# The level decays of a chunked recurrence: products of block decays in place of exponentials of differences of a running sum

## The chip, the cores and the metric

One core of one Trainium2 chip runs the whole program. The metric is the device time of one execution in microseconds, the median of several runs; before the change it is 2116.34 us, the median of 3 runs (2110.68 to 2116.36).

## The reference

Two transformer blocks run on 512 tokens of width 1024: a first block with sparse attention, latent attention and a gated feed-forward, and a second block of two layers. The change touches the first layer of the second block, an HGRN2 mixer with 8 heads of 128 key and 128 value dimensions. Cut to what matters:

```
log_f = log_sigmoid(f) ;  k = sigmoid(-f) ;  q = silu(q)          # lb is zero for this layer
per chunk of 128 frames, per head:
    b = cumsum(log_f)                                              # running sum of log decays
    scores[t, s] = sum_d q[t, d] * exp(b[t, d] - b[s, d]) * k[s, d]    for s <= t, else 0
    o = (q * exp(b)) @ state + scores @ v
    state = exp(b_last) * state + (k * exp(b_last - b))^T @ v
o = rms_norm(o) * silu(g), then @ w_out
```

The decay depends on the dimension d as well as on t and s, so the scores are no plain product of two matrices.

## The kernel before, in words

Every tile has features or dimensions on the 128 partitions and the 512 tokens on the free axis. Weights are float32 and are split into a high part on ACT (`whi`, line 431) and a rest on DVE (`wlo`, line 435); every dense product is three matmuls (`mm3`, line 481). `take` (line 443) issues the split of a block of weights three blocks ahead (`LOOK_SPLIT`) and its DMA five ahead.

The scores of a chunk are built by levels h = 64, 32, 16, 8, 4, 2, 1. At level h the tokens form pairs of blocks of length h, and the level covers the queries of a pair's second block against the keys of its first. There the decay is a product of two factors that meet at the middle of the pair, exp(b[t] - b[mid]) on the query and exp(b[mid] - b[s]) on the key, so that a matmul over d gives the scores. The diagonal needs no decay.

`hz` (line 1941) takes the projections of a head: for `f` it makes `zf` (the key), and a scan on DVE (line 1950, with the mask `scan` that is loaded at line 1926) makes the running sum `b`. `hrec` (line 1975) then does a head. It makes `kd` = k exp(b_last - b) (POOL line 1982, ACT 1984, DVE 1985), `eb` = exp(b) (ACT 1987) and `qe` = q exp(b) (DVE 1989); four matmuls `ps<-zq,zf` for the diagonal go through a predicated copy into the score tile `sc` (line 1994). `kd` is transposed on PE (line 2000) and copied back by ACT (2001). Then come the seven levels, the largest first, all from `b`, `k` and `q`. `level` (line 2005) has two subtractions on POOL (2027, 2028; one for h = 1, 2012), one exponential on ACT (2029; 2013) and two multiplications on DVE (2030, 2031; 2014, 2015) into a tile `lx`. `levmm` (line 2034) has four matmuls `ps<-lx` (one against a tile of ones for h = 1) and puts the result into `sc`, with ACT copies for h = 64 and 32 (2049, 2054) and predicated copies on DVE otherwise (2056). `vi,kd` makes the states (`st`, line 2077, scaled by a column of `eb`), `vi,sc` and `st,qe` the output of the head, and `qe` is used once more for the normalised output.

The order of the work: `hrec` is a generator that yields after each level; two of them (even and odd heads) are woven with the generator `hgrn_dense` of projections by the rates of `RATE_H` (`weave_g`, line 261). A scheduler of the framework then orders each engine's queue. Tiles of 128x512 come from a list of free slots, first in first out (`get`, `put`, lines 302 and 316).

Of the kernel before, what the change touches and what calls it, by code (L numbers as in the profile page):

```python
# [19 lines left out]
P = 128  # L20
T = 512
# [54 lines left out]
def _constants():  # L76
# [30 lines left out]
    sm = np.ones((P, T), np.float32)  # L107
    sm[:, ::P] = 0.0
    c["c_scan"] = sm
# [834 lines left out]
def _emit(s):  # L944
# [980 lines left out]
    scanm = s.get("scan")  # L1925
    nc.sync.dma_start(scanm, A["c_scan"])
# [48 lines left out]
    def hrec(hd):  # L1975
        q, k, b, g = (qfg.pop((hd, n)) for n in "qkbg")
# [12 lines left out]
        V.tensor_tensor(qe, eb, q, op=ALU.mult)  # L1989
# [15 lines left out]
        def level(i, h):  # L2005
            nb = T // (2 * h)
            x = s.get("lx")
            b4, k4, q4 = (y.rearrange("p (n e t) -> p n e t", e=2, t=h) for y in (b, k, q))
            if h == 1:
                x0 = x[:, 0:256]  # L2010
                x3 = x0.rearrange("p (n t) -> p n t", t=1)
                G.tensor_tensor(x3, b4[:, :, 1, :], b4[:, :, 0, :], op=ALU.subtract)
                S.activation(x0, x0, AF.Exp)
                V.tensor_tensor(x3, x3, k4[:, :, 0, :], op=ALU.mult)
                V.tensor_tensor(x3, x3, q4[:, :, 1, :], op=ALU.mult)
                lev[i] = x
                return
            mid = b4[:, :, 0, h - 1:h].to_broadcast([P, nb, h])
            if h == 32:
                x5 = x.rearrange("p (b e n t) -> p e b n t", b=NT, e=2, n=2)  # L2020
                x4 = [x5[:, e] for e in range(2)]
                v5 = lambda y: y.rearrange("p (b n) t -> p b n t", b=NT)
            else:
                x5 = x.rearrange("p (n e t) -> p e n t", e=2, t=h)
                x4 = [x5[:, e] for e in range(2)]
                v5 = lambda y: y
# [5 lines left out]
            lev[i] = x  # L2032

        def levmm(i, h):
            x = lev.pop(i)
            ps = s.ps()
            if h == 1:
                s.mm(ps[:, 0:256], s.ones, x[:, 0:256], True, True)
            for tb in range(NT if h > 1 else 0):
                xb = x[:, tb * P:(tb + 1) * P]  # L2040
                if h >= 32:
                    s.mm(ps[0:64, 64 * tb:64 * tb + 64], xb[:, 0:64], xb[:, 64:128], True, True)
                else:
                    r = xb.rearrange("p (n e t) -> p n e t", e=2, t=h)[:, :, 1, :]
                    s.mm(ps[:, 64 * tb:64 * tb + 64].rearrange("p (n t) -> p n t", t=h), xb, r, True, True)
# [41 lines left out]
        s.put(kd, eb, st, q, k, b)  # L2087
# [55 lines left out]
    s.put(rbc, scanm, *SC, *VI[0], *VI[1], *masks)  # L2143
# [286 lines left out]
```

## Time and profile before

| | before |
|---|---|
| median of 3 runs | 2116.34 us |
| the profiled execution's own time | 2109.22 us |
| its span | 2107.4 us |
| mean granted clock of TensorE, of full speed | 0.989 |
| PE busy | 2064.9 us (98%) |
| DVE busy | 1641.5 us (78%) |
| ACT busy | 1170.4 us (56%) |
| POOL busy | 138.5 us (7%) |

The span is the time from the first to the last instruction that the profiler saw; the own time has what lies around it. PE are matmuls, PEld their weight loads, DVE VectorE, ACT ScalarE, POOL GpSimd, SP the engine that issues most DMAs. A busy share is one of the whole span and hides stages with other limits. The HGRN stage's recurrence lies between 865 and 1140 us.

### The profile page before, as it was taken

To read this page: it belongs to the slowest core of one execution; us is meant where nothing else is said; L and a number is where in the kernel's file an instruction comes from. 1 tells how busy PE (TensorE), PEld (TensorE's weight loads), DVE (VectorE), ACT (ScalarE), POOL (GpSimd) and SP (SyncE) were. 2 spreads that over 40 slices of the span, in tenths; PEclk is the share of its full clock that TensorE was granted. 3 is DMA by queue.
4 is the path that set the end of the run, shared out by engine and by line. 5 is a ranking of instruction groups with operands and counts; after the bars stand their busy time and mean duration, and the time that the engine had idled before them with its cause. 6 is when DMAs were issued, how large, how long until landed. Compare 5 with 4: busy or idle time off the path is not lost.

```text
span 2107.4 us, 30853 instructions
## 1 busy us (share of the span) xinstructions
PE 2064.9 (98%) x11194; PEld 1748.6 (83%) x11194; DVE 1641.5 (78%) x3285; ACT 1170.4 (56%) x2174; POOL 138.5 (7%) x256
## 2 busy tenths in 40 slices
PE   9999999999999999899989999999999999999998
PEld 8788877988888889798878988888888879888886
DVE  7786698799687897977996967667887677666768
ACT  5565676465444474645664645445656565554453
POOL 0000001100000000422440000000000000000000
PEclk9999999999999999999999999999999999999999
DMA  7123166433424252222122442343563433434342
GB/s 229 41 61 100 58 176 222 155 122 106 142 91 139 101 170 91 86 70 71 61 91 90 150 159 101 131 140 112 193 201 112 141 124 114 148 109 153 108 139 92
DMA packets 106359, 258.22 MB, mean 123 GB/s; under 512 B 10944, under 2 KB 31280, under 8 KB 106208
## 3 DMA queue, kind: packets, MB, share of 16 engines
q1 hardware_dynamic: 106208, 256.27, 36.8%
q8 instruction: 88, 1.44, 0.3%
q14 instruction: 63, 0.52, 0.1%
HBM read 227.61 MB, written 24.16 MB: 119 GB/s over the span
## 4 chain that ended last, share of the span: by engine, by line
PE 47%; DVE 5%; POOL 2%; issue 1%; ACT 1%; DMA 1%; SPq 0%; DVEq 0%; POOLq 0%; ACTq 0%
PE ps L479 45%; POOL lx L2028 1%; POOL lx L2027 1%; DVE wlo L435 1%; PE s L479 1%; PE o L479 1%; DMA dtab<-rexp 1%; PE rms L479 0%; DVE lx L2030 0%; DVE lx L2031 0%; DMA raw<-in_mup 0%; ACT whi L431 0%; DVE p L2313 0%; DVE rt L684 0%; DVE xr L1758 0%
## 5 line engine op out<-in xcount | busy, mean ns | idle before, releaser
L479 PE MATMUL ps<-ah,whi 128*128 128x512 f32 (+1 forms) x1812 | 677.3, 375 | 1.8 <-ACT whi L431 1.2
L479 PE MATMUL ps<-al,whi 128*128 128x512 f32 (+1 forms) x1812 | 670.5, 370 | 1.9 <-DVE al L641 1.4
L479 PE MATMUL ps<-ah,wlo 128*128 128x512 f32 (+1 forms) x1812 | 668.1, 369 | 0.0
L431 ACT CAST whi<-raw 128x1024 fp32r<-128x1024 f32 (+3 forms) x283 | 280.4, 995 | 302.2 <-PE ps L479 286.6
L435 DVE TENSOR_TENSOR wlo<-raw,whi 128x1024 fp32r<-128x1024 f32 (+3 forms) x283 | 332.7, 1178 | 137.9 <-ACT whi L431 137.2
L479 PEld LDWEIGHTS ps<-ah,whi 128*128 128x128 f32 x1812 | 341.0, 189 | 59.8 <-ACT whi L431 1.8
L479 PEld LDWEIGHTS ps<-ah,wlo 128*128 128x128 f32 x1812 | 341.1, 188 | 59.3 <-DVE wlo L435 0.2
L479 PEld LDWEIGHTS ps<-al,whi 128*128 128x128 f32 x1812 | 341.8, 189 | 57.3 <-DVE al L641 2.3
L479 PE MATMUL ps<-whi,ah 128*128 128x512 f32 (+2 forms) x816 | 291.7, 358 | 2.1 <-DVE am L871 1.5
L479 PE MATMUL ps<-wlo,ah 128*128 128x512 f32 (+2 forms) x816 | 290.6, 356 | 1.4 <-DVE wlo L435 1.4
L479 PE MATMUL ps<-whi,al 128*128 128x512 f32 (+2 forms) x816 | 290.2, 356 | 0.0
L479 PEld LDWEIGHTS ps<-whi,ah 128*128 128x128 f32 x816 | 154.5, 189 | 27.2 <-DVE am L871 1.7
L479 PEld LDWEIGHTS ps<-wlo,ah 128*128 128x128 f32 x816 | 154.8, 190 | 26.0 <-DVE wlo L435 2.2
L479 PEld LDWEIGHTS ps<-whi,al 128*128 128x128 f32 x816 | 154.5, 190 | 23.9
L431 ACT CAST whi<-t 128x1024 fp32r<-128x1024 f32 x66 | 67.9, 1029 | 95.6 <-DVE t L394 56.0
L873 ACT ACTIVATE p<-p,am 128x128 f32<-128x128 f32 (+3 forms) x160 | 88.5, 554 | 37.1 <-DVE am L871 36.1
L435 DVE TENSOR_TENSOR wlo<-t,whi 128x1024 fp32r<-128x1024 f32 x66 | 79.0, 1198 | 38.4 <-ACT whi L431 34.7
L637 ACT CAST ah<-u 128x512 fp32r<-128x512 f32 x97 | 59.6, 619 | 46.3 <-DVE u L1720 30.1
L435 DVE TENSOR_TENSOR wlo<-b,whi 128x1024 fp32r<-128x1024 f32 (+1 forms) x44 | 52.5, 1197 | 35.4 <-ACT whi L431 35.4
L479 PE MATMUL ps<-ah,wh 128*128 128x256 f32 x256 | 73.1, 285 | 0.0
L1667 DVE TENSOR_TENSOR C<-C,ps 128x512 f32<-128x512 f32 x112 | 72.5, 681 | 0.7 <-PE ps L479 0.7
L696 DVE TENSOR_TENSOR ss<-ss,sq 128x512 f32<-128x512 f32 (+1 forms) x90 | 51.8, 575 | 27.0 <-ACT sq L695 25.7
(359 smaller groups left out, 3322.1 us busy)
## 6 DMA issues: line engine op xcount, KB each, us to landing
raw<-in_mup SPq DMA_DIRECT2D x64, 512.0 KB, 3.3
raw<-in_mdn SPq DMA_DIRECT2D x64, 512.0 KB, 3.2
raw<-in_up SPq DMA_DIRECT2D x44, 512.0 KB, 4.2
b<-in_mdn SPq DMA_DIRECT2D x32, 512.0 KB, 3.3
raw<-in_win SPq DMA_DIRECT2D x26, 512.0 KB, 3.8
raw<-in_awin SPq DMA_DIRECT2D x24, 512.0 KB, 3.2
raw<-in_down SPq DMA_DIRECT2D x20, 512.0 KB, 3.3
xsp<-x SPq DMA_DIRECT2D x32, 256.0 KB, 2.3
```

The lines of the kernel that those rows point to most:

```text
L431: self.whi_ins = self.nc.scalar.copy(hi[:, :e], raw[:, :e])
L435: eng.tensor_tensor(lo[:, d], raw[:, d], hi[:, d], op=ALU.subtract)
L479: self.nc.tensor.matmul(ps, l, r, start=first, stop=last, skip_group_check=skip)
L637: nc.scalar.copy(hi, src)
L696: nc.vector.tensor_tensor(ss[:, c], ss[:, c], t[:, c], op=ALU.add)
L873: nc.scalar.activation(d, d, AF.Exp, scale=-1.0, bias=m[:, qb:qb + 1], accum_out=sm[:, qb:qb + 1])
L1667: V.tensor_tensor(C[i, j, tb], C[i, j, tb], pss[tb], op=ALU.add)
L2027: G.tensor_tensor(x4[1], v5(b4[:, :, 1, :]), v5(mid), op=ALU.subtract)
L2028: G.tensor_tensor(x4[0], v5(mid), v5(b4[:, :, 0, :]), op=ALU.subtract)
```

## The change

The running sum `b` is gone, with its scan, its mask (a constant, a load and a tile), and every exponential of a difference. `hz` keeps `f` itself, exp(log_f), in the tile `ls`. `hrec` builds up from the smallest level. The decays of blocks come from DVE: `dec[2h]` is the product of neighbouring pairs of `dec[h]`, seven products of 256, 128, ..., 4 elements into a tile `dt` (line 1990 of the changed kernel). Two running operands start as K = k and Q = f q. At each level h, K's first block of a pair is multiplied by the decay of the second block and Q's second block by the decay of the first (DVE, lines 2004 and 2005, into new tiles `Kd` and `Qd`), and the other halves are copied by ACT (lines 2006, 2007). The matmuls of a level (`ps<-Qd,Kd`) use K and Q as they were ahead of its step; at h = 32 the weights are 96 columns (before: 64). After the level 64 K is k exp(b_last - b) and Q is q exp(b), so that the separate `kd`, `eb` and `qe` go; the transposes of K (line 2051) and their copy (2053) now stand behind the last level. The level h = 1 has a product `x1` of its own (line 1993). POOL has no work left in the recurrence.

```
@@ _constants, loads
-    sm = np.ones((P, T), np.float32)
-    sm[:, ::P] = 0.0
-    c["c_scan"] = sm
...
-    scanm = s.get("scan")
-    nc.sync.dma_start(scanm, A["c_scan"])
@@ hz
             S.activation(z, z, AF.Exp)
-            b = s.get("b")
-            V.tensor_tensor_scan(b, scanm, e, 0.0, ALU.mult, ALU.add)
-            qfg[hd, "k"], qfg[hd, "b"] = z, b
+            S.activation(e, e, AF.Exp)
+            qfg[hd, "k"], qfg[hd, "f"] = z, e
@@ hrec
-        kd = s.get("kd")
-        b3 = b.rearrange("p (a t) -> p a t", a=NT)
-        G.tensor_tensor(kd.rearrange("p (a t) -> p a t", a=NT), b3[:, :, P - 1:P].to_broadcast([P, NT, P]), b3,
-                        op=ALU.subtract)
-        S.activation(kd, kd, AF.Exp)
-        V.tensor_tensor(kd, kd, k, op=ALU.mult)
-        eb = s.get("eb")
-        S.activation(eb, b, AF.Exp)
-        qe = s.get("qe")
-        V.tensor_tensor(qe, eb, q, op=ALU.mult)
...
-        kps = s.ps()
-        for tb in range(3):
-            c = slice(tb * P, (tb + 1) * P)
-            nc.tensor.transpose(kps[:, c], kd[:, c], s.ident)
-        S.copy(kd[:, 0:384], kps[:, 0:384])
-        s.pput(kps)
-        lev = {}
+        K, Q = k, s.get("Qd")
+        V.tensor_tensor(Q, f, q, op=ALU.mult)
+        s.put(q)
+        dt = s.get("dt")
+        dec, o = {1: f}, 0
+        for h in (1, 2, 4, 8, 16, 32, 64):
+            n = T // (2 * h)
+            dec[2 * h] = dt[:, o:o + n]
+            d3 = dec[h].rearrange("p (n e) -> p n e", e=2)
+            V.tensor_tensor(dec[2 * h], d3[:, :, 0], d3[:, :, 1], op=ALU.mult)
+            o += n
+        x1 = s.get("x1")
+        V.tensor_tensor(x1[:, 0:256], k[:, 0::2], Q[:, 1::2], op=ALU.mult)
+        yield
+        lev = deque()
...
-            G.tensor_tensor(x4[1], v5(b4[:, :, 1, :]), v5(mid), op=ALU.subtract)
-            G.tensor_tensor(x4[0], v5(mid), v5(b4[:, :, 0, :]), op=ALU.subtract)
-            S.activation(x, x, AF.Exp)
-            V.tensor_tensor(x4[0], x4[0], v5(k4[:, :, 0, :]), op=ALU.mult)
-            V.tensor_tensor(x4[1], x4[1], v5(q4[:, :, 1, :]), op=ALU.mult)
-            lev[i] = x
+            V.tensor_tensor(k2[:, :, 0, :], kb[:, :, 0, :], d3[:, :, 1:2].to_broadcast([P, nb, h]), op=ALU.mult)
+            V.tensor_tensor(q2[:, :, 1, :], qb[:, :, 1, :], d3[:, :, 0:1].to_broadcast([P, nb, h]), op=ALU.mult)
+            S.copy(k2[:, :, 1, :], kb[:, :, 1, :])
+            S.copy(q2[:, :, 0, :], qb[:, :, 0, :])
+            lev.append((h, K, Q))
+            K, Q = K2, Q2
...
-                    s.mm(ps[0:64, 64 * tb:64 * tb + 64], xb[:, 0:64], xb[:, 64:128], True, True)
+                    e = P - h
+                    s.mm(ps[0:e, 64 * tb:64 * tb + 64].rearrange("p (n t) -> p n t", t=h), kb[:, c][:, 0:e],
+                         q4[:, :, 1, :], True, True)
...
-        hs = (64, 32, 16, 8, 4, 2, 1)
-        for i, h in enumerate(hs):
-            level(i, h)
+        for i, h in enumerate((1, 2, 4, 8, 16, 32, 64)):
+            level(h)
             if i:
-                levmm(i - 1, hs[i - 1])
+                levmm()
             yield
+        s.put(f)
+        kps = s.ps()
+        for tb in range(3):
+            c = slice(tb * P, (tb + 1) * P)
+            nc.tensor.transpose(kps[:, c], K[:, c], s.ident)
+        kd, qe = K, Q
+        S.copy(kd[:, 0:384], kps[:, 0:384])
+        s.pput(kps)
...
-        levmm(6, 1)
+        levmm()
...
-            V.scalar_tensor_tensor(st[:, tb * P:(tb + 1) * P], st[:, (tb - 1) * P:tb * P], eb[:, tb * P + P - 1:tb * P + P],
+            V.scalar_tensor_tensor(st[:, tb * P:(tb + 1) * P], st[:, (tb - 1) * P:tb * P], dec[128][:, tb:tb + 1],
```

How the queues stand. First DVE in the opening, where the first head's levels begin; before, the level multiplications of head 0 in their order (`zf` is the key, `zq` the query):

```order
L1985 TENSOR_TENSOR kd<-kd,zf 128x512
L1938 SCALAR_TENSOR_TENSOR ls<-zf,ls 128x512
L1989 TENSOR_TENSOR qe<-eb,zq 128x512
L1947 TENSOR_TENSOR zf<-ls,zf 128x512
L1950 SCALAR_TENSOR_TENSOR b<-scan,ls 128x512
L2030 TENSOR_TENSOR lx<-lx,zf 128x4x64
L2031 TENSOR_TENSOR lx<-lx,zq 128x4x64
L2030 TENSOR_TENSOR lx<-lx,zf 128x4x64
L2031 TENSOR_TENSOR lx<-lx,zq 128x4x64
L435 TENSOR_TENSOR wlo<-raw,whi 128x1024
```

and after the change, the same place:

```order
L1990 TENSOR_TENSOR dt<-dt 128x64
L2004 TENSOR_TENSOR Kd<-zf,ls 128x256
L1990 TENSOR_TENSOR dt<-dt 128x32
L2005 TENSOR_TENSOR Qd<-Qd,ls 128x256
L1990 TENSOR_TENSOR dt<-dt 128x16
L2004 TENSOR_TENSOR Kd<-Kd,dt 128x128x2
L1990 TENSOR_TENSOR dt<-dt 128x8
L2005 TENSOR_TENSOR Qd<-Qd,dt 128x128x2
L1990 TENSOR_TENSOR dt<-dt 128x4
L2038 COPY_PREDICATED sc<-mask,ps 128x256
L432 TENSOR_TENSOR wlo<-raw,whi 128x1024
```

The small products `dt` stand between the multiplications of the first two levels, and each level's multiplication now reads the tile that the level ahead of it wrote.

Second ACT, somewhat later, where both heads' levels run; before:

```order
L1984 ACTIVATE kd<-kd 128x512
L1987 ACTIVATE eb<-b 128x512
L2029 ACTIVATE lx<-lx 128x512 x2
L431 CAST whi<-raw 128x1024
L2001 COPY kd<-ps 128x384
L2029 ACTIVATE lx<-lx 128x512 x2
```

and after:

```order
L2053 COPY Kd<-ps 128x384
L2006 COPY Kd<-Kd 128x32x8
L2007 COPY Qd<-Qd 128x32x8
L2006 COPY Kd<-Kd 128x16x16
L2007 COPY Qd<-Qd 128x16x16
L428 CAST whi<-raw 128x1024
L2006 COPY Kd<-Kd 128x8x32
L2007 COPY Qd<-Qd 128x8x32
```

Two copies of half the size stand where one exponential stood, and a weight cast can stand between the copies of one level and the next.

Third PE at head 6, near the end of the stage; before, where the levels 16 to 2 of that head follow each other without dense matmuls (`ident,qe` are transposes of another head's output, `vi,sc` its score product):

```order
L479 MATMUL ps<-lx 128x64 x16
L479 MATMUL ps<-vi,kd 128x128 x3
L479 MATMUL ps<-lx,ones 128x256
L2106 MATMUL ps<-ident,qe 128x128 x2
L479 MATMUL ps<-zq,zf 128x128 x2
```

and after:

```order
L476 MATMUL ps<-Qd,Kd 128x64 x12
L476 MATMUL ps<-Qd,Kd 96x64 x4
L2051 MATMUL ps<-ident,Kd 128x128 x3
L476 MATMUL ps<-Qd,Kd 64x64 x4
L476 MATMUL ps<-zq,zf 128x128
L476 MATMUL ps<-vi,Kd 128x128 x3
L2095 MATMUL ps<-ident,Qd 128x128 x4
```

The transposes of `Kd` moved behind the last level, and five matmuls stand between them and `vi,Kd`, which reads their copy.

## Rows read from the trace of the kernel before

**Rows 1.** The page's busy times: engine, us, share of the span, instructions.
```profile
PE 2064.9 (98%) x11194; PEld 1748.6 (83%) x11194; DVE 1641.5 (78%) x3285; ACT 1170.4 (56%) x2174; POOL 138.5 (7%) x256
```
**Rows 2.** Busy time by stretch: length, PE, PEld, DVE, ACT, POOL, granted clock, DMA share, GB/s.
```profile
865.00:1140.00 275.00, 259.48 (x1609) 226.74 (x1609) 231.54 (x451) 158.70 (x335) 102.40 (x112) 0.95 0.21 70
870.00:900.00 30.00, 22.69 (x149) 20.53 (x148) 29.97 (x38) 18.75 (x37) 26.69 (x28) 0.80 0.07 24
1050.00:1080.00 30.00, 27.07 (x135) 22.89 (x134) 27.96 (x59) 20.82 (x41) 6.82 (x8) 0.89 0.20 71
1080.00:1110.00 30.00, 26.09 (x156) 21.44 (x155) 29.31 (x58) 19.62 (x43) 15.47 (x17) 0.95 0.35 115
1110.00:1125.00 15.00, 15.00 (x102) 13.49 (x102) 12.36 (x40) 4.95 (x17) 3.38 (x4) 0.88 0.30 88
```
**Rows 3.** PE timeline: start, us, line, operation, [idle before and what ended it].
```profile
876.24 0.52 PE L2000 MATMUL ps<-ident,kd 128*128 128x128 f32 x3 [1.62 <-DVE kd L1985]
882.41 1.11 PE L479 MATMUL ps<-lx 128*64 128x64 f32 x8 [1.96 <-DVE lx L2031]
...
1056.39 1.22 PE L479 MATMUL ps<-vi,sc 128*128 128x128 f32 x4 [2.93 <-DVE sc L2056]
...
1106.79 1.22 PE L479 MATMUL ps<-lx,ones 128*128 128x256 f32 x2 [3.69 <-DVE sc L2056]
```
**Rows 4.** DVE and POOL timelines around 896 us, POOL's last subtraction of heads 0 and 1.
```profile
894.42 0.83 DVE L2031 TENSOR_TENSOR lx<-lx,zq 128x256 f32<-128x256 f32 x1
895.18 0.42 DVE L2056 COPY_PREDICATED sc<-mask,ps 128x256 f32<-128x256 uint32 x1
...
898.24 0.41 DVE L2030 TENSOR_TENSOR lx<-lx,zf 128x256 f32<-128x256 f32 x1
898.57 0.41 DVE L2031 TENSOR_TENSOR lx<-lx,zq 128x256 f32<-128x256 f32 x1
...
896.44 0.79 POOL L2012 TENSOR_TENSOR lx<-b 128x256 f32<-128x256 f32 x1
```
**Rows 5.** Groups of DVE instructions, 865 to 1140 us: count | busy us, mean ns | idle before.
```profile
L435 DVE TENSOR_TENSOR wlo<-raw,whi 128x1024 fp32r<-128x1024 f32 x28 | 38.0, 1357 | 4.8 <-ACT whi L431 4.6
L2030 DVE TENSOR_TENSOR lx<-lx,zf 128x256 f32<-128x256 f32 x48 | 28.1, 586 | 0.6 <-ACT lx L2029 0.6
L2031 DVE TENSOR_TENSOR lx<-lx,zq 128x256 f32<-128x256 f32 x48 | 26.3, 548 | 0.0
L1950 DVE TENSOR_TENSOR_SCAN b<-scan,ls 128x512 f32<-128x512 f32 x8 | 10.1, 1267 | 0.0
L1985 DVE TENSOR_TENSOR kd<-kd,zf 128x512 f32<-128x512 f32 x8 | 7.3, 916 | 0.1
```
**Rows 6.** Groups of DVE instructions, 600 to 868 us, where POOL does no subtraction.
```profile
L435 DVE TENSOR_TENSOR wlo<-raw,whi 128x1024 fp32r<-128x1024 f32 x36 | 44.0, 1222 | 14.8 <-ACT whi L431 14.8
L707 DVE TENSOR_TENSOR x<-x,y 128x256 f32<-128x256 f32 x16 | 6.4, 419 | 0.0
L683 DVE TENSOR_TENSOR rt<-ry 128x2 f32<-128x2 f32 x12 | 1.9, 160 | 0.2
```
**Rows 7.** Groups of ACT instructions, 865 to 1140 us.
```profile
L2029 ACT ACTIVATE lx<-lx 128x512 f32<-128x512 f32 x48 | 29.9, 629 | 21.9 <-POOL lx L2028 21.7
L2013 ACT ACTIVATE lx<-lx 128x256 f32<-128x256 f32 x8 | 3.3, 408 | 0.4 <-POOL lx L2012 0.4
```
**Rows 8.** PE timeline: a level's group of matmuls with 128 and with 64 columns.
```profile
1075.32 1.00 PE L479 MATMUL ps<-lx 128*128 128x64 f32 x8
...
1093.86 0.68 PE L479 MATMUL ps<-lx 128*64 128x64 f32 x8
```
**Rows 9.** ACT timeline: the copy behind the transposes of 876.24.
```profile
876.80 0.48 ACT L2001 COPY kd<-ps 128x384 f32<-128x384 f32 x1 [1.10 <-PE ps L2000]
```
**Rows 10.** Waits, 828 to 1145 us: us in total, times, longest.
```profile
ACT whi L431 <- PE ps L479: 24.9, 9, 5.2
DVE wlo L435 <- ACT whi L431: 7.5, 7, 4.0
```

More of the change, by code (lines that the diff above doesn't have):

```diff
@@ L1955, in hz @@
             qfg[hd, n] = z
-        s.put(e)
+            s.put(e)
     def hproj(hd):
@@ L1975, in hrec @@
     def hrec(hd):
[L1976 removed]
+        q, k, f, g = (qfg.pop((hd, n)) for n in "qkfg")
         v = lambda tb: VI[hd // 4][tb][:, (hd % 4) * P:(hd % 4) * P + P]
         sc = SC[hd % len(SC)]
[L1980 to L1989 removed]
         dps = s.ps()
@@ L1995, in hrec @@
         s.pput(dps)
-        yield
-        kps = s.ps()
-        for tb in range(3):
-            c = slice(tb * P, (tb + 1) * P)
-            nc.tensor.transpose(kps[:, c], kd[:, c], s.ident)
-        S.copy(kd[:, 0:384], kps[:, 0:384])
-        s.pput(kps)
-        lev = {}
-        def level(i, h):
-            nb = T // (2 * h)
[L2007 to L2015, printed above, removed]
-                lev[i] = x
[L2017 to L2026, printed above, removed]
-            G.tensor_tensor(x4[1], v5(b4[:, :, 1, :]), v5(mid), op=ALU.subtract)
-            G.tensor_tensor(x4[0], v5(mid), v5(b4[:, :, 0, :]), op=ALU.subtract)
-            S.activation(x, x, AF.Exp)
-            V.tensor_tensor(x4[0], x4[0], v5(k4[:, :, 0, :]), op=ALU.mult)
-            V.tensor_tensor(x4[1], x4[1], v5(q4[:, :, 1, :]), op=ALU.mult)
-            lev[i] = x
@@ new lines, in hrec, with level @@
+        V.tensor_tensor(x1[:, 0:256], k[:, 0::2], Q[:, 1::2], op=ALU.mult)
+        yield
+        lev = deque()
+        def level(h):
+            nonlocal K, Q
+            K2, Q2 = s.get("Kd"), s.get("Qd")
+            kb, qb, k2, q2 = (y.rearrange("p (n e t) -> p n e t", e=2, t=h) for y in (K, Q, K2, Q2))
+            d3 = dec[h].rearrange("p (n e) -> p n e", e=2)
+            nb = T // (2 * h)
+            V.tensor_tensor(k2[:, :, 0, :], kb[:, :, 0, :], d3[:, :, 1:2].to_broadcast([P, nb, h]), op=ALU.mult)
[4 more added lines that the diff above has]
+            K, Q = K2, Q2
@@ L2036, in levmm @@
+        def levmm():
+            h, kb, qb = lev.popleft()
+            i = (64, 32, 16, 8, 4, 2, 1).index(h)
             ps = s.ps()
             if h == 1:
-                s.mm(ps[:, 0:256], s.ones, x[:, 0:256], True, True)
+                s.mm(ps[:, 0:256], s.ones, x1[:, 0:256], True, True)
+                s.put(x1)
             for tb in range(NT if h > 1 else 0):
-                xb = x[:, tb * P:(tb + 1) * P]
+                c = slice(tb * P, (tb + 1) * P)
+                q4 = qb[:, c].rearrange("p (n e t) -> p n e t", e=2, t=h)
@@ L2053, in levmm @@
                 for n in range(2):
-                    S.copy(d5[64 * n:64 * n + 32, :, n, 1, :], s5[32 * n:32 * n + 32, :, n, :])
+                    S.copy(d5[64 * n:64 * n + 32, :, n, 1, :], s5[64 * n:64 * n + 32, :, n, :])
             else:
                 V.copy_predicated(dst, masks[(i - 1) // 2].bitcast(U32)[:, 256 * ((i - 1) % 2):256 * ((i - 1) % 2) + 256].rearrange("p (n t) -> p n t", t=h), src)
-            s.put(x)
+            s.put(kb, qb)
             s.pput(ps)
-        hs = (64, 32, 16, 8, 4, 2, 1)
-        for i, h in enumerate(hs):
-            level(i, h)
+        for i, h in enumerate((1, 2, 4, 8, 16, 32, 64)):
+            level(h)
             if i:
-                levmm(i - 1, hs[i - 1])
+                levmm()
             yield
+        s.put(f)
+        kps = s.ps()
+        for tb in range(3):
+            c = slice(tb * P, (tb + 1) * P)
+            nc.tensor.transpose(kps[:, c], K[:, c], s.ident)
+        kd, qe = K, Q
+        S.copy(kd[:, 0:384], kps[:, 0:384])
+        s.pput(kps)
         while ("v", hd // 4) not in done:
@@ L2086, in hrec @@
                 s.mm(ops[:, c], qe[:, c], st[:, (tb - 1) * P:tb * P], False, True)
-        s.put(kd, eb, st, q, k, b)
+        s.put(kd, st, dt)
         yield
@@ L2142, in _emit @@
     s.putacts(acts)
-    s.put(rbc, scanm, *SC, *VI[0], *VI[1], *masks)
+    s.put(rbc, *SC, *VI[0], *VI[1], *masks)
     ho = [ho[i] for i in range(8)]
```

6 lines of the change are left out of this document (2 added, 4 removed).

## The prediction

> **What bounds the kernel now.** I read the page's busy times first, then busy time by stretch, then the PE timeline of the stretches that show a gap, then what ended each gap, and last the DVE and POOL timelines beside it. Over the whole span PE is busy 98% [rows 1]: the kernel is a chain of matmuls, and an edit in the HGRN stage is worth what PE loses there. By stretch, the part of the stage in which POOL works is 865 to 1140 us: PE is busy 259.48 of 275 us at a mean granted clock of 0.95, DVE 231.54, ACT 158.70, POOL 102.40 [rows 2]. So PE loses 15.5 us to gaps, and more to the clock. The losses lie in three places: 870 to 900 (7.3 us idle, clock 0.80, and DVE busy 29.97 of 30), 1050 to 1080 (2.9 us, 0.89), and 1080 to 1125 (3.9 us, 0.95 and 0.88) [rows 2]; the other 1.4 us of gaps are scattered. [...] Each of these gaps ends with DVE: `kd`, `lx`, and twice the predicated copy into `sc` [rows 3].
>
> Why is DVE late? Its level multiplications, 128x256 with both inputs in SBUF, take 0.83 us while POOL subtracts, and 0.41 us four microseconds later, when POOL's last subtraction of the two first heads (896.44) is over; the predicated copy between them, whose data comes from PSUM, takes 0.42 us in the middle of POOL's work [rows 4]. So POOL's 102 us nearly double what DVE does meanwhile.
>
> **The change part by part.** All sums are against the profiled execution: its span 2107.4 us, its own time 2109.22 us, 7.1 us under the median of the three runs (2116.34).
>
> POOL: all 112 subtractions go, 102.40 us [rows 2]. Its DMA issues and its memsets are as before; nothing waits for POOL in this stage any more.
>
> DVE: out go the scan (10.1), the `kd` and `qe` multiplications (7.3 for `kd`, twice that for both), the level multiplications (28.1 + 26.3) [rows 5] and the sixteen of h=1 (about 0.42 each, 6.7): 86 us. In come, at undisturbed prices, 112 level multiplications at 0.42 (47.0), eight for `x1` (3.4) and eight of 128x512 for `Q`; between 0.419 for 256 and 1.222 for 1024 elements [rows 6] I put those at 0.69 (5.5). The 56 decay products (256 elements, halved six times) are not in the trace; the bounds are 0.160 us (a 128x2 operation) and 0.419 [rows 6], so 9.0 to 23.5 us; on the straight line between these two rows a head's seven are 1.6 us, 12.9 in all, and I take that, since six of the seven are small. The sum is 69 us, 17 us less than before (6 to 21). The weight splits `wlo`, 28 in the stage, fall from 1357 to 1222 ns [rows 5, 6], 3.8 us, and other two-input operations with them. DVE ends near 205 of 275 us; it is then no longer beside PE's 259 but well under it.
>
> [...]
>
> ACT: out go 48 exponentials of 512 (29.9), eight of 256 (408 ns each, 3.3) and 16 for `kd` and `eb` (at the same 629 ns, 10.1) [rows 7]: 43.3 us. In come eight exponentials of `f` (5.0) and 112 strided copies of 256 elements. A strided SBUF copy of this size is not in the trace; the bounds are 0.32 us (two thirds of a copy of 384 from PSUM, 0.48 [rows 9]) and 629 ns (512 elements [rows 7]), 36 to 70 us; I take the exponential of equal size, 408 ns, 45.7 us, the nearest row. ACT gains 7.4 us (-2 to +32) and stays under 191 of 275 us. Under PE this costs nothing; if the cover went, it would cost those 7 us.
>
> PE: the matmul count stays. The h=32 groups get 96 columns for 64; a group of four takes 0.68 us with 64 and 1.00 us with 128 [rows 8], and half of the difference on eight heads is 1.3 us (0 to 2.6).
>
> New waits. First, levels were independent and now follow each other: a level's multiplication (0.42) and its copy on ACT (0.41) come before the next, 0.83 us, while DVE has two multiplications in it that follow each other at 0.33 us [rows 4], 0.67 us. That leaves 0.16 us idle a level, 9 us of DVE over 56 levels; cover: DVE at 205. PE's group of a level takes 1.0 us, so even where nothing else stands between groups the chain keeps pace. Second, `K` is transposed only behind the last level, and `vi,Kd` follows with five to eight matmuls between (about 0.9 to 1.4 us) in heads 2 to 7; the copy ends 0.5 us behind the transposes when ACT is free [rows 9], so this costs 0 to 4 us, where a weight cast stands in front; I take 1. Queues: no DMA moves past work on SP; the load of the scan mask (256 KB) goes and its successors move up, under other work, worth nothing.
>
> Gain: the stage's loss is 15.5 us of gaps, and on busy PE time 0.20 of 22.69, 0.11 of 27.07, 0.05 of 26.09 and 0.12 of 15.00 us [rows 2], 10.6 us of clock: 26 us at most. Opening (870 to 900), 11.8 us: DVE's work from the first `Qd` to the end of head 1's levels is 11 x 0.69 + 42 x 0.42 + 4 x 1.22 + 2.3 = 32 us, so it is through by about 903, where it now is busy without a break and still behind at 900; PE keeps two waits of a chain step each and a little clock, 3.5; gain 8.3. Scattered gaps, 1.4: gain 1.2. Middle (1050 to 1080), 5.9: DVE has its slack back; gain 5.0. Tail (1080 to 1125), 7.0: heads 6 and 7 have few dense matmuls left between their groups, and their chains start only when the last projections are done; I take half, 3.5. Together 18.0, less 1.3 and 1.0: **16 us**. The span goes to 2091, the own time to 2093, the median to **2100 us**.
>
> **Rivals.**
> *More.* All 26 us come back: 2090 us. For it: DVE falls far enough; against: two waits of 1.6 and 2.0 us were followed by the lower clock [rows 3], and the opening keeps such waits. It is the low end.
> *No gain.* The chain takes the place of the contention: in the opening and the tail PE waits for fourteen steps of 0.83 us and more, and keeps what it loses there; only the middle and the scattered gaps gain, 7.3 less 2.3: 5 us, 2111 us. Against: by the order the opening has 164 dense matmuls beside the chains of two heads. A sub-case, that POOL was not what slows DVE, so that the change doesn't do what it is built on, gives the same; the 0.42 us of the copy from PSUM and the end of the slow rows with POOL's last one speak against it. [...]
> *Slower.* ACT's queue is in order, and its weight casts wait nine times, up to 5.2 us and 24.9 us in all, for PE to free a weight buffer [rows 10]. Level copies now stand behind these casts; DVE then stands at the next level's multiplication with a weight split `wlo` behind it, and PE runs out of weights. If all of it came through, 24.9 - 16 = 9 us are lost: 2125 us. The point is two thirds of these waits; below, the gain wins. Against: three blocks of weights are split ahead (`LOOK_SPLIT`), and of all these waits DVE's weight splits saw 7.5 us [rows 10].
>
> **How the numbers follow.** The gain, of any size above 6 us (0.3%, about what a measurement of this kernel tells from no change): 0.70, of which the full one 0.15. No gain: 0.17. Slower: 0.13. The range goes from 2086, 4 us under the full gain (2090), since the runs of before themselves lie up to 5.7 us under their median, to 2118, which holds the no-gain case with the 0.3% above it and leaves out most of the slower one.
>
> **What would show it.** Right: DVE multiplications of 128x256 at 0.41 to 0.43 us throughout; DVE near 205 and ACT near 166 us in the stage; gaps of PE in 870 to 900 below 3 us with a clock above 0.9; copies near 0.41 us; `vi,Kd` rows without a wait of a microsecond. Wrong: PE gaps that end with ACT's `Kd` or `Qd` copy or with DVE `Qd` on every level (no gain), or with DVE `wlo` while ACT waits for PE (slower); copies of 0.6 us.

## The result and the profile after

The changed kernel takes **2090.41 us** (median of 4 runs, 2088.2 to 2091.22); the kernel before, with the runs made beside it, 2114.94 us. The ratio is 0.9886, 95% interval [0.9868, 0.9903]: 24 us, by the interval 20.5 to 28, are gained. The forecast was 2100 (2086 to 2118), faster with 0.70. So the direction and the mechanism held and the size was too small; the rival that had all 26 us come back (2090) was nearer. Most of the miss of 9.6 us lies between span and median: the forecast of the span, 2091, was off by 1.6 only.

The profiled execution of the changed kernel has a span of 2089.4 us and its own time is 2091.22, against 2107.4 and 2109.22 before. Its busy times, for [rows 1]:

```profile
PE 2057.2 (98%) x11194; PEld 1744.2 (83%) x11194; DVE 1605.5 (77%) x3333; ACT 1174.1 (56%) x2222; POOL 35.9 (2%) x144
```

POOL lost its 102 us, ACT got 4 us more, DVE has 48 instructions more and 36 us less. The same by stretch, for [rows 2] (length, PE, PEld, DVE, ACT, POOL, granted clock, DMA share, GB/s):

```profile
870.00:900.00 30.00, 28.48 (x228) 27.53 (x227) 28.18 (x69) 23.51 (x54) 0.00 (x0) 0.94 0.16 54
900.00:1080.00 180.00, 180.00 (x1128) 158.76 (x1127) 138.64 (x338) 118.99 (x274) 0.00 (x0) 1.00 0.23 77
1080.00:1110.00 30.00, 29.59 (x211) 25.95 (x210) 23.41 (x85) 13.51 (x45) 0.00 (x0) 1.00 0.32 106
```

In the opening PE is idle for 1.5 us instead of 7.3, at clock 0.94 instead of 0.80; in 900 to 1080 it never stops, where it was idle for 4.2 us before, 2.9 of them at 1050 to 1080; in the tail it is idle for 0.4 us at full clock. All that PE still waits for in this part, 865 to 1140 us (for [rows 3]; in total, times, longest):

```profile
PE ps L476 <- DVE x L1993: 1.0, 1, 1.0
PE ps L476 <- DVE dt L1990: 0.4, 1, 0.4
PE ps L476 <- ACT sc L2036: 0.3, 1, 0.3
```

DVE's groups, 865 to 1105 us, for [rows 5], and ACT's copies, for [rows 7]:

```profile
L432 DVE TENSOR_TENSOR wlo<-raw,whi 128x1024 fp32r<-128x1024 f32 x29 | 35.5, 1224 | 13.6 <-ACT whi L428 13.4
L2004 DVE TENSOR_TENSOR Kd<-Kd,dt 128x256 f32<-128x256 f32 x48 | 20.3, 424 | 0.7 <-ACT Kd L2006 0.7
L2005 DVE TENSOR_TENSOR Qd<-Qd,dt 128x256 f32<-128x256 f32 x48 | 20.2, 421 | 0.1
...
L2007 ACT COPY Qd<-Qd 128x256 f32<-128x256 f32 x56 | 23.1, 412 | 6.9 <-DVE Qd L2005 4.4 <-DVE zq L1948 0.8 <-DVE rt L681 0.6
L2006 ACT COPY Kd<-Kd 128x256 f32<-128x256 f32 x48 | 19.6, 408 | 4.8 <-DVE Kd L2004 3.1 <-DVE dt L1990 0.6 <-DVE rt L680 0.6
```

The multiplications take 0.42 us throughout (0.55 to 0.59 in the mean before), `wlo` 1224 ns (1357), the copies 0.41: each as the forecast had it.

For comparing kernels one measure is used from here on, the **stage**: from ACT's first `ls` activation on head 0's `zf` to the last transpose of head 7's output. These lines are the busy times over exactly that stretch, of the kernel before and of the changed one:

```profile
864.60:1134.20 269.60, 254.08 (x1582) 222.47 (x1581) 229.21 (x448) 155.31 (x329) 102.40 (x112) 0.95 0.21 70
```
```profile
867.30:1109.60 242.30, 240.37 (x1574) 214.26 (x1573) 192.77 (x496) 158.71 (x378) 0.00 (x0) 0.99 0.23 78
```

The stage is 27.3 us shorter. In these two executions the span is only 18.0 shorter: the changed one enters the stage 2.7 us later, and after it PE waits 3.2 us instead of 1.5 for a row maximum of the next attention stage, at a lower clock behind it (0.50 from 1541.5 to 1545 us; at the same place before, 1562 to 1566, 1.00). That wait came out at 1.3 and at 3.2 us in two profiles of the same changed kernel, with the 1.5 of before between them, so nothing shows it to be an effect of the change.

### The profile page after: what moved, and what is told of

The parts are those of the page before. It is cut to its first block, busy times and chain, and to the rows that moved or that the text cites. A ratio compares the mean times of both kernels' runs of the same rounds, so it can differ in the third digit from the quotient of the medians.

```text
span 2089.4 us, 30898 instructions
## 1 busy us (share of the span) xinstructions
PE 2057.2 (98%) x11194; PEld 1744.2 (83%) x11194; DVE 1605.5 (77%) x3333; ACT 1174.1 (56%) x2222; POOL 35.9 (2%) x144
## 4 chain that ended last, share of the span: by engine, by line
PE 88%; DVE 6%; ACT 3%; DMA 2%; issue 1%; SPq 0%; DVEq 0%; ACTq 0%; POOL 0%; POOLq 0%
PE ps L476 80%; PE s L476 3%; PE o L476 2%; PE pt L902 1%; DVE wlo L432 1%; PE rms L476 1%; ACT whi L428 1%; DMA dtab<-rexp 0%; PE rms L660 0%; DMA raw<-in_win 0%; DMA raw<-in_mup 0%; DMA raw<-in_pleg 0%; DVE p L2302 0%; DVE p L868 0%; DVE xr L1755 0%
```

## The experiments

| kernel | median us | ratio to before, 95% interval | stage us |
|---|---|---|---|
| before | 2112 to 2115 | 1 | 269.6 |
| changed | 2090.41 | 0.9886 [0.9868, 0.9903] | 242.3 |
| changed, POOL's subtractions back as dead work | 2130.84 | 1.0074 [1.0057, 1.0091] | 281.5 |
| changed, dead copies on POOL | 2099.81 | 0.9928 [0.9913, 0.9942] | 257.2 |
| before, no subtractions | 2085.87 | 0.987 [0.9849, 0.9891] | 242.1 |
| before, subtractions on DVE | 2109.47 | 0.9978 [0.9965, 0.999] | 267.3 |
| changed, dead memsets on POOL | 2094.41 | 0.9909 [0.9889, 0.9928] | 243.0 |
| changed, ACT's copies doubled | 2093.41 | 0.9911 [0.989, 0.9931] | 247.5 |
| changed, 112 dead DVE multiplications | 2104.78 | 0.9956 [0.9941, 0.9971] | 257.2 |
| changed, half copies on POOL | 2093.28 | 0.9907 [0.9889, 0.9925] | 248.2 |
| changed, again | 2090.45 | 0.9889 [0.9875, 0.9904] | 243.9 |
| changed, `x1` ahead of the decay products | 2087.41 | 0.9874 [0.9859, 0.9889] | 240.1 |
| changed, two table loads early | 2087.56 | 0.9878 [0.9863, 0.9893] | 240.7 |
| changed, both | 2087.68 | 0.9872 [0.9856, 0.9888] | 240.2 |

The theory: POOL's subtractions slowed DVE's SBUF operations, DVE came late, PE got gaps, and the clock fell behind them (in the kernel before 1.00 from 870 to 880 us and 0.50 from 884 to 888, behind the two waits at the head of [rows 3]). The rivals: the gain is that of cheaper or fewer instructions, or of the new order of the levels.

**POOL's subtractions put back, as dead work**

```diff
+        G.tensor_tensor(p3, f3[:, :, P - 1:P].to_broadcast([P, NT, P]), f3, op=ALU.subtract)
         K, Q = k, s.get("Qd")
...
+            if h > 1:
+                G.tensor_tensor(x4[:, :, 1, :], w4[:, :, 1, :], mid, op=ALU.subtract)
+            G.tensor_tensor(x4[:, :, 0, :], mid, w4[:, :, 1 if h == 1 else 0, :], op=ALU.subtract)
             V.tensor_tensor(k2[:, :, 0, :], kb[:, :, 0, :], ...
```

> The changed kernel with GpSimd's 112 subtractions put back as dead work: per head one of 128x512 and thirteen of 128x256, two SBUF inputs each, that read f and write a scratch tile that nobody reads. No engine waits for them. Theory (POOL's two-input work slows VectorE's SBUF operations, VectorE is then late, PE gets gaps and a lower clock): VectorE's 128x256 multiplications take 0.8 us while POOL works, VectorE's busy time of the stage goes from 198 back over 225 us, PE's idle time and the lower clock return in the opening, and the time is 2098 to 2114. Rival (the gain came from fewer VectorE instructions or from the new order of the levels): 2087 to 2093, multiplications at 0.42 us.

Measured: 2130.84 us, 40 more than the changed kernel and 16 more than the kernel before. The stage:

```profile
865.80:1147.30 281.50, 251.85 (x1571) 222.63 (x1570) 230.99 (x496) 160.55 (x377) 98.34 (x112) 0.94 0.21 67
```

The three longest of PE's waits in it:

```profile
PE ps L476 <- ACT Kd L2062: 16.7, 3, 8.3
PE ps L476 <- DVE Qd L2014: 4.2, 3, 1.6
PE ps L476 <- DVE x L1996: 3.3, 2, 2.1
```

And DVE's timeline around 887 us (start, us, line, operation):

```profile
886.30 0.83 DVE L2013 TENSOR_TENSOR Kd<-Kd,dt 128x256 f32<-128x256 f32 x1
887.05 0.84 DVE L2014 TENSOR_TENSOR Qd<-Qd,dt 128x256 f32<-128x256 f32 x1
...
890.48 0.42 DVE L2047 COPY_PREDICATED sc<-mask,ps 128x256 f32<-128x256 uint32 x1
```

Work that nobody waits for costs all of the gain and more, and 0.83 us is back, beside 0.42 for the copy from PSUM, as in [rows 4]. Not every multiplication is lengthened: in the mean of the stage `Kd` takes 0.47 us and `Qd` 0.49. DVE's busy time rises by 38 us, from 192.8 to 231.0, with the same 496 instructions. So the contention is shown. The size was outside what the theory expected, and the waits tell why: the largest is for the copy `Kd` behind the transposes, which in the new order stand behind the last level. With DVE late, that chain is worse than the old order: the same DVE time as before (231 and 229 us), and a stage 12 us longer.

**One-input copies on POOL, at the same places**

```diff
-            G.tensor_tensor(x4[:, :, 0, :], mid, w4[:, :, 1 if h == 1 else 0, :], op=ALU.subtract)
+            G.tensor_copy(x4[:, :, 0, :], w4[:, :, 0, :])
```

(against the kernel above; the two other subtractions likewise)

> The changed kernel with dead GpSimd work of the same places and sizes as in the run with the subtractions put back, but as copies with one SBUF input (one of 128x512 and thirteen of 128x256 a head, from f into a scratch tile). Theory in the form that only two-input work of GpSimd contends: VectorE's multiplications stay at 0.42 us and the time at 2087 to 2093. Rival (any GpSimd traffic on SBUF slows VectorE): 0.6 us or more, 2095 to 2112.

Measured: 2099.81 us, 9 more than the changed kernel. The stage:

```profile
865.60:1122.80 257.20, 248.85 (x1570) 219.92 (x1569) 206.59 (x496) 160.14 (x377) 75.78 (x112) 0.96 0.22 74
```

DVE's timeline at POOL's last copy of the first two heads, and that copy in POOL's:

```profile
893.57 0.61 DVE L2012 TENSOR_TENSOR Kd<-Kd,dt 128x256 f32<-128x256 f32 x1
894.10 0.61 DVE L2013 TENSOR_TENSOR Qd<-Qd,dt 128x256 f32<-128x256 f32 x1
...
894.97 0.41 DVE L2012 TENSOR_TENSOR Kd<-Kd,dt 128x256 f32<-128x256 f32 x1
...
893.85 0.59 POOL L2011 COPY pw<-ls 128x256 f32<-128x256 f32 x1
```

The form "only two-input work contends" falls: beside a copy with one SBUF input these multiplications take 0.61 us, and 0.41 as soon as the last copy has ended. Beside subtractions with two inputs it was 0.83. An overlap does not always lengthen the multiplication: at 891.21 and 891.82 us it took 0.41, and POOL's copies from 891.23 and 891.83 took 0.65 and 0.67, others 0.40. The lengthened ones are the smaller part, as the mean over the stage shows:

```profile
L2012 DVE TENSOR_TENSOR Kd<-Kd,dt 128x256 f32<-128x256 f32 x48 | 21.4, 446 | 0.4 <-ACT Kd L2014 0.3
```

DVE's sum rises by 14 us where the subtractions added 38.

**The kernel before without the subtractions**

```diff
-            G.tensor_tensor(x4[1], v5(b4[:, :, 1, :]), v5(mid), op=ALU.subtract)
-            G.tensor_tensor(x4[0], v5(mid), v5(b4[:, :, 0, :]), op=ALU.subtract)
-            S.activation(x, x, AF.Exp)
+            S.activation(x, b, AF.Exp)
```

(and so for h=1 and `kd`)

> The kernel before, with GpSimd's 112 subtractions left out: ScalarE's exponentials read the running sum b instead of the differences, so the decays are other numbers; all of VectorE's and PE's work of before stays, the scan too. Theory (contention): VectorE's level multiplications at 0.42 us, its busy time of the stage falls from 231 to about 190 us, PE's gaps go, and the time is 2087 to 2096, as fast as the changed kernel or nearly. Rival (fewer instructions, or the chain of levels): 2105 to 2116.

Measured: 2085.87 us, a microsecond below the theory's range. The stage:

```profile
867.10:1109.20 242.10, 240.60 (x1581) 212.10 (x1580) 195.27 (x448) 152.70 (x329) 0.00 (x0) 1.00 0.24 78
```

DVE's groups of level multiplications in it:

```profile
L2026 DVE TENSOR_TENSOR lx<-lx,zq 128x256 f32<-128x256 f32 x48 | 20.1, 418 | 0.0
L2025 DVE TENSOR_TENSOR lx<-lx,zf 128x256 f32<-128x256 f32 x48 | 20.0, 416 | 0.1
```

With the subtractions gone the whole gain is there. With the scan, the exponentials and the old order all in place, the stage takes 242.1 us, against 242.3 in the changed kernel. DVE's 448 instructions fall from 229.2 to 195.3 us: **contention cost DVE 34 us**. The swap of DVE's operations that the change makes is worth the other 2.5 us (195.3 to 192.8), and nothing in the time. The interval overlaps with the changed kernel's: the level chain, the copies and the 96 columns have no net price here that these runs can see. By itself this run doesn't tell contention from another cause: it also takes POOL's step out of the chain of a level, for which ACT waited 21.7 us before [rows 7]. The dead subtractions above tell them apart, since nobody waits for those.

**The kernel before with the subtractions on DVE**

```diff
-            G.tensor_tensor(x4[1], v5(b4[:, :, 1, :]), v5(mid), op=ALU.subtract)
+            V.tensor_tensor(x4[1], v5(b4[:, :, 1, :]), v5(mid), op=ALU.subtract)
```

(all 112)

> The kernel before, with the 112 subtractions moved from GpSimd to VectorE: nothing leaves the program, VectorE gets 104 operations of 128x256 and eight of 128x512 more, about 40 us by the step of 0.33 us from start to start, and nothing else touches SBUF meanwhile. Theory (contention costs VectorE more than the subtractions themselves): VectorE's busy time of the stage is 225 to 240 us, no more than before, and the time is 2092 to 2108, faster than before though VectorE got 112 instructions more. Rival (VectorE's own load sets the gaps): 2115 to 2140, slower than before.

Measured: 2109.47 us, faster than before by 0.1 to 0.35%, and above the range of the theory. The stage, and the stretch in which it lost most:

```profile
867.90:1135.20 267.30, 254.42 (x1576) 222.70 (x1575) 232.13 (x560) 157.43 (x329) 0.00 (x0) 0.94 0.21 69
...
1100.00:1130.00 30.00, 23.60 (x121) 20.36 (x121) 22.25 (x65) 9.13 (x24) 0.00 (x0) 0.72 0.20 62
```

DVE does 112 operations more than in the kernel before in 3 us more (232.1 against 229.2): POOL's help had spared DVE next to nothing. But the stage is hardly shorter either, by 2.3 us. I had expected the gaps to be smaller because the contention was gone; DVE's time alone brings them back, here in the tail, where the clock falls to 0.72.

**Memsets on POOL**

```diff
+            G.tensor_copy(PS[:, 0:1], d3[:, 0, 0:1])
+            G.memset(PW[:, 0:256], 0.0)
+            if h > 1:
+                G.memset(PW[:, 256:512], 0.0)
```

> The changed kernel with dead GpSimd work that reads almost nothing: at the places of the former subtractions, memsets of 128x256 (of 128x512 once a head) into a scratch tile, each level's pair held back by a copy of 128x1 that reads a decay. Theory in the form the two runs so far suggest (VectorE waits for GpSimd instructions that read SBUF, whole instruction by whole instruction: 0.41 us longer beside two inputs, 0.19 beside one): multiplications at 0.42 us, 2087 to 2093. Rival (GpSimd's writes contend as well): multiplications of 0.5 us or more where memsets run, 2094 to 2105.

Measured: 2094.41 us, the rival's number, but with a stage of 243.0, no longer than the changed kernel's. The test isn't the one meant: nothing held the memsets themselves back, and all 112 ran at 831 to 862 us, ahead of the stage. What they did there is of use. POOL's memsets over the whole run, and DVE's groups of 831 to 863 us:

```profile
L2009 POOL MEMSET pw<- 128x256 f32 x56 | 17.7, 316 | 0.5
...
L704 DVE TENSOR_TENSOR x<-x,y 128x256 f32<-128x256 f32 x13 | 5.2, 416 | 0.0
L1897 DVE TENSOR_SCALAR y<-y,cols 128x256 f32<-128x256 f32 x2 | 4.4, 2216 | 0.0
```

Two-input operations of DVE are untouched beside memsets (416 ns; 419 at the same place in the changed kernel). A `tensor_scalar` with one SBUF input takes 2216 ns in the mean of two, where it took 349 in the changed kernel. PE waits 3.0 us there for a small operation of DVE, a wait that the changed kernel doesn't have; that it makes up most of the 4 us of this run was not tried, and the intervals overlap. So in these runs which of DVE's operations suffered depended on what POOL did.

**ACT's copies doubled**

```diff
             S.copy(q2[:, :, 0, :], qb[:, :, 0, :])
+            S.copy(w4[:, :, 1, :], kb[:, :, 1, :])
+            S.copy(w4[:, :, 0, :], qb[:, :, 0, :])
```

> The changed kernel with every half copy on ScalarE done a second time, into a scratch tile that nobody reads: 112 more of 0.41 us, ScalarE's busy time of the stage from 164 to about 209 of 251 us. Theory (ScalarE's 7 us were priced at nothing because they lie beside PE's work): 2088 to 2096, at most the opening gains a microsecond or two of gaps. Rival (the copies stand in the chain from level to level and ScalarE's queue is in order, so what ScalarE does more comes out at the end): 2100 to 2135.

Measured: 2093.41 us; the interval overlaps with the changed kernel's. The stage:

```profile
867.60:1115.10 247.50, 244.94 (x1573) 217.28 (x1571) 192.16 (x496) 189.38 (x489) 0.00 (x0) 0.97 0.23 76
```

ACT's busy time goes from 158.7 to 189.4 us in the stage (its mean per copy, 0.41 us, stays), the stage is 5 us longer in this execution, and the median moves by about 3 us, within the range of the theory. The 7 us that ACT was charged with are worth nothing measurable.

**112 more multiplications on DVE**

```diff
+            for e in range(2):
+                V.tensor_tensor(w4[:, :, e, :], f4[:, :, e, :], f4[:, :, 1 - e, :], op=ALU.mult)
             lev.append((h, K, Q))
```

> The changed kernel with two dead 128x256 multiplications more on VectorE per level, two SBUF inputs each, behind the level's own: 112 x 0.33 us from start to start, 37 us, so that VectorE has about 235 of 251 us, as much as in the kernel before, with GpSimd silent. Theory (VectorE's lateness counts, whatever makes it late; contention was one way to get it): PE's gaps come back in the opening and the tail, with the lower clock, 2102 to 2118. Rival (contention does something that VectorE's load alone does not): 2088 to 2096.

Measured: 2104.78 us, 14 more than the changed kernel. The stage and the tail:

```profile
866.60:1123.80 257.20, 247.76 (x1573) 218.39 (x1572) 225.29 (x608) 160.43 (x377) 0.00 (x0) 0.97 0.22 74
...
1080.00:1110.00 30.00, 24.01 (x152) 20.61 (x150) 28.60 (x101) 15.33 (x42) 0.00 (x0) 0.89 0.24 76
```

DVE's lateness is what counts, without POOL too. It isn't DVE's sum alone, though: one-input copies on POOL cost the same 257.2 us of stage with DVE at 206.6 us, and here it takes 225.3. The dead multiplications are spread over all levels behind the real ones; the contention strikes just when a level is computed. That this is the reason was not tried.

**The half copies on POOL instead of ACT**

```diff
-            S.copy(k2[:, :, 1, :], kb[:, :, 1, :])
-            S.copy(q2[:, :, 0, :], qb[:, :, 0, :])
+            G.tensor_copy(k2[:, :, 1, :], kb[:, :, 1, :])
+            G.tensor_copy(q2[:, :, 0, :], qb[:, :, 0, :])
```

> The changed kernel with its 112 half copies on GpSimd instead of ScalarE: ScalarE has 46 us less, but each copy reads SBUF on GpSimd between two VectorE multiplications of the chain. Theory (GpSimd's reads and VectorE's two-input operations exclude each other): copies of 0.4 to 1.0 us, multiplications at 0.6, and as the copies now stand in the chain, PE waits in opening and tail: 2098 to 2125. Rival (the load that matters is ScalarE's, and one-input copies are harmless): 2084 to 2092.

Measured: 2093.28 us, below the theory's range and a little above the rival's. The stage:

```profile
868.70:1116.90 248.20, 244.62 (x1567) 216.54 (x1566) 200.21 (x496) 123.72 (x266) 64.59 (x112) 0.97 0.23 76
```

Of the groups of DVE and POOL, one multiplication and one copy:

```profile
L2004 DVE TENSOR_TENSOR Kd<-Kd,dt 128x256 f32<-128x256 f32 x48 | 22.2, 462 | 0.0
L2007 POOL COPY Qd<-Qd 128x256 f32<-128x256 f32 x56 | 32.0, 572 | 31.9 <-DVE Qd L2005 11.0 <-DVE dt L1990 6.5 <-DVE zq L1948 5.3
```

The multiplication takes 0.46 us in the mean, not 0.6: I had taken the price of a meeting for that of every multiplication. Beside the dead copies the mean was no higher, 0.45. DVE's sum rises by 7 us instead of 14 because other operations are lengthened less (`ls<-zg,ls` 698 ns here and 795 there, 688 in the changed kernel); why is not shown. ACT's 35 us less buy nothing.

**What is left: two edits on the changed kernel**

> The changed kernel once more, unaltered, as the yardstick for the three kernels beside it: 2087 to 2093 us.

> The changed kernel with each head's seven decay products taken out of the row ahead of x1 and issued one by one behind the level that precedes their use; the same instructions in another order on VectorE. Theory (what is left in the opening is VectorE's queue: waits of 0.4 us for dt and 1.0 us for x1, and 1.6 us of clock behind them): x1 and the first level come up to 0.9 us earlier per head, the time is 1 to 3 us under the yardstick. Rival (the opening is bound by the projections, and a product now stands in front of the next level's multiplication): no difference of more than 1 us, or up to 2 us slower.

> The changed kernel with one edit in the next attention stage: the loads of the first two bias tables (dtab) are issued ahead of the eight spills of x on SP's queue, instead of behind them. Theory (the 6 us by which the whole span gained less than the HGRN stage did lie there: PE waited 3.2 us for a row maximum whose table landed late, and ran at a lower clock behind it): the wait goes to under 1.5 us and the time is 2 to 6 us under the yardstick. Rival (the loads only change places with the spills that the same stretch needs): within 1.5 us of the yardstick.

> Both edits, the decay products behind the levels and the two early table loads. Theory: the gains add, 3 to 8 us under the yardstick, 2081 to 2088 us. Rival: no more than the better of the two.

The first edit, on the levels:

```diff
-        for h in (1, 2, 4, 8, 16, 32, 64):
-            n = T // (2 * h)
-            dec[2 * h] = dt[:, o:o + n]
...
             S.copy(q2[:, :, 0, :], qb[:, :, 0, :])
+            dec[2 * h] = dt[:, od:od + nb]
+            V.tensor_tensor(dec[2 * h], d3[:, :, 0], d3[:, :, 1], op=ALU.mult)
```

The second, in the attention stage that follows (and `dhead` uses the two tables if they are there):

```diff
+    for i in range(2):
+        load_tab(i)
     spill(xs)
```

Measured: the yardstick 2090.45 us; `x1` first 2087.41; tables early 2087.56; both 2087.68. Each is about 3 us under the yardstick, all intervals overlap with its, and the gains don't add, as the rival of the last had it. All three beat the kernel before; that one beats the changed kernel isn't shown. The opening of the yardstick, of `x1` first, and of tables early, which has the yardstick's HGRN code:

```profile
870.00:900.00 30.00, 28.48 (x208) 27.21 (x207) 28.23 (x67) 24.02 (x53) 0.00 (x0) 0.89 0.13 42
```
```profile
870.00:900.00 30.00, 29.00 (x248) 28.40 (x248) 28.43 (x70) 24.91 (x58) 0.00 (x0) 1.00 0.17 54
```
```profile
870.00:900.00 30.00, 28.47 (x242) 27.61 (x241) 28.77 (x72) 25.29 (x57) 0.00 (x0) 1.00 0.17 54
```

With `x1` first the wait for `dt` is gone and PE is idle for 1.0 us instead of 1.5. The larger part of the difference is the clock, and that came out at 0.94, 0.89 and 1.00 in three executions of the same instructions with the same idle time. Their stages took 242.3, 243.9 and 240.7 us: the 240.1 of `x1` first lies within that spread. With the tables early PE's 1 to 3 us wait for the row maximum is gone; with both edits PE instead waits 2.8 us for the weight load `raw<-in_kvk`, which the same queue had to bring.

## Why the forecast was right, and what was too small

**What bounds, and the cause.** Right. PE's loss was in the gaps that end with DVE, DVE was late because of POOL, and taking POOL's subtractions out of the old kernel gives the whole gain. The sub-case that POOL was not the cause falls with the first and third experiment. What DVE loses differs by the pair: a two-input 128x256 multiplication took 0.83 us beside POOL's subtractions and 0.61 beside its copies, 0.41 behind the last of either; beside memsets the two-input addition kept 416 ns, while the one-input operation took 2216 instead of 349. By what mechanism POOL holds DVE up, no run here shows.

**DVE's sum.** The forecast wrote 17 us less for the operations and 3.8 for `wlo`, near 205 us; measured over the stage it is 36.4 less, 192.8. The direction was right and the size short. What the forecast priced came out as it wrote it, durations added up as there: 86.6 us go, 68.7 come in, and `wlo` loses 3.7. The term that it left without a sum is "other two-input operations with them": all other operations together are 11.7 us shorter, where the step to 205 leaves about 6. Two of them over the stage, before and after:

```profile
L1938 DVE SCALAR_TENSOR_TENSOR ls<-zg,ls 128x512 f32<-128x512 f32 x8 | 7.8, 971 | 0.1
L1954 DVE TENSOR_TENSOR zg<-zg,ls 128x512 f32<-128x512 f32 x8 | 7.5, 936 | 0.9 <-ACT ls L1953 0.9
```
```profile
L1933 DVE SCALAR_TENSOR_TENSOR ls<-zg,ls 128x512 f32<-128x512 f32 x8 | 5.5, 688 | 0.3 <-ACT ls L1932 0.2
L1948 DVE TENSOR_TENSOR zg<-zg,ls 128x512 f32<-128x512 f32 x8 | 5.5, 682 | 0.0
```

The last 3.1 us are overlap, which a busy time counts once and a sum of durations twice: 28.7 us before, 31.8 after. The decay products have a part in that. Their durations add up to 12.6 us, as the forecast's 12.9 had it, but short operations of DVE overlap, as the timeline of the changed kernel shows:

```profile
1083.97 0.17 DVE L1990 TENSOR_TENSOR dt<-dt 128x16 f32<-128x16 f32 x1
1084.06 0.42 DVE L1993 TENSOR_TENSOR x<-zf,Qd 128x256 f32<-128x256 f32 x1
...
1085.76 0.15 DVE L1990 TENSOR_TENSOR dt<-dt 128x4 f32<-128x4 f32 x1
1085.83 0.42 DVE L2005 TENSOR_TENSOR Qd<-Qd,ls 128x256 f32<-128x256 f32 x1
```

From start to start they take 0.09 and 0.07 us, and the seven of this head 0.33, 0.20, 0.13, 0.11, 0.09, 0.07 and 0.07, 1.0 us: 8 us for eight heads. The forecast's 12.9 was worked out from durations, 160 and 419 ns [rows 6]; what such an operation takes from DVE's time, where the next follows without a wait, is the step.

**ACT's sum.** 7.4 us more were written; it is 3.4 (155.3 to 158.7), with copies of 0.41 as taken: these overlap as well, since 112 more of them added 30.7 us, 0.27 each. Its price of nothing is right: 31 us more on ACT moved the median by 3, inside the noise.

**PE's gains, place by place.** Idle time and clock, added in slices of 10 us of both traces:

| place | lost before | lost after | gain | forecast |
|---|---|---|---|---|
| opening | 12.8 | 3.2 | 9.6 | 8.3 |
| scattered | 1.4 | 0 | 1.4 | 1.2 |
| middle | 5.7 | 0 | 5.7 | 5.0 |
| tail | 6.7 | 0.4 | 6.3 | 3.5 |
| sum | 26.6 | 3.6 | 23.0 | 18.0 |

The step that failed is the tail: "heads 6 and 7 have few dense matmuls left between their groups", and so "I take half, 3.5". The premise is right, the halving is not. The old kernel without subtractions has the order of before on PE, with the same six dense matmuls (128x512) among the last heads' groups. First PE before, up to its wait of 3.69 us for the copy into `sc` (the last row of [rows 3]); then the same place in that run, where the wait is gone:

```profile
1098.70 3.68 PE L479 MATMUL ps<-lx 128*128 128x64 f32 x32
1102.22 0.88 PE L479 MATMUL ps<-vi,kd 128*128 128x128 f32 x6
```
```profile
1081.52 3.68 PE L479 MATMUL ps<-lx 128*128 128x64 f32 x32
1085.04 0.88 PE L479 MATMUL ps<-vi,kd 128*128 128x128 f32 x6
1085.76 0.60 PE L479 MATMUL ps<-lx,ones 128*128 128x256 f32 x2
```

From 1098.7 to 1121.5 us PE was busy for 18.89 of 22.80 us at a clock of 0.85; the same groups take 15.10 us in the other run (1081.5 to 1096.6), all of it busy, at 1.00. In the changed kernel, too, there are six dense matmuls from 1082.6 to 1097.5, and PE is idle for 0.28 us. So with DVE on time the last levels need no cover; the forecast had said so itself, "even where nothing else stands between groups the chain keeps pace", and then left half of the gain out. Where DVE is late again the tail loses again: 6.4 us idle at 0.72 with the subtractions on DVE, 6.0 at 0.89 with the dead multiplications.

The opening's kept loss, 3.5 us, came out at 3.2, but at 4.7 and 1.5 by the same sum in two other executions of the same code (the changed kernel again, and the tables early), with the clock as the only difference: so close an agreement is luck; the forecast of its gain was short mostly because the clock was still down until 910 (0.90 from 900 to 910 us), which its sum over 870 to 900 left out.

**The charges.** 1.3 us for h=32's columns and 1.0 for `vi,Kd` were taken off. The first is there in its own rows: from 867 to 1110 us the matmuls with 96 columns are busy for 7.1 us, as many with 64 columns for 5.4. It doesn't show in the stage, where the old kernel without subtractions has 240.6 us of busy PE against 240.4. The second isn't seen: no `vi,Kd` waits in the changed kernel. Its place was right, however: with DVE late it is the largest wait of all, 16.7 us.

**The sum and the medians.** The tail's 2.8 us, the opening's 1.3, 0.9 at the other two places and the charges of 2.3 lead from the forecast's 15.7 us to the 23.0 of the table. The stage is 27.3 us shorter; the other 4.3 stay open, and the clock is given in hundredths. That the medians come out near this, 24.5 us apart, is in part luck: the two profiled executions, from which all these sums are taken, are 18.0 us apart in span, and a span of 2089.4 us is 1.6 under the forecast's 2091. To get to its 2100 the forecast added the 7.1 us by which the profiled execution of before lay under its median. That of the changed kernel lies 0.8 us above its own.

**The rivals.** *No gain* by a chain of 0.83 us per level: the chain is there, but DVE stood for only 0.7 us in all for ACT's copy of `Kd` (its group above) where the forecast allowed 9, and no wait of PE ends with it. *Slower* by ACT's casts holding level copies: ACT's `whi` still waits for PE, 30.7 us in 19 times between 828 and 1125 us (24.9 in nine before [rows 10]), and DVE's `wlo` behind it 15.0; PE waits for neither in the stage. A cast does hold a ready copy, as the level 32 of head 1 shows: DVE multiplies from its operand `Kd` at 898.75 us, ACT is idle for 1.32 us until `whi` starts at 899.95, and the copy from the same operand starts at 900.90.

## What to carry to other kernels

An engine that is off every chain can still set the time, by what it does to another engine's operations (the dead subtractions: multiplications of 0.83 us for 0.41, and 40 us of time): look for one operation and shape with two durations, and see which engine falls silent where the shorter one begins. Moving work from a nearly full engine to a free one is no help if the free one then blocks the full one for as long; taking the work away is (2112 to 2115 us with the subtractions on POOL, 2109.47 with them on DVE, 2085.87 without). Price every operation that the cause touches, not only those that the edit touches, and cost short operations by the time from start to start (a head's seven products here: 1.0 us, and 1.6 by durations). Before writing off half of a gap because nothing covers it, ask whether the chain, once it is on time, still needs cover (the tail here got back 6.3 of 6.7 us).

## What the runs showed of the hardware that was not expected

- GpSimd copies with a single SBUF input lengthen VectorE's two-input 128x256 multiplication from 0.41 to 0.61 us (893.57 and 894.10 us of that run); subtractions with two inputs lengthen it to 0.83 (886.30 us).
- GpSimd memsets leave VectorE's two-input 128x256 addition at 0.416 us, but lengthen a one-input 128x256 `tensor_scalar` from 0.349 to 2.216 us, in the mean of two.
- The granted clock of the opening was 0.94, 0.89 and 1.00 in three executions of the same instructions, with PE idle for 1.5 us in each.
